# Batched matmul with addend: the weight in one transfer, a strided turn, regrouped stores, and two loads of x ahead of the addends

## The chip, the cores and the metric

The kernel runs on one core of one Trainium2 chip. The metric is device time in microseconds (us); a run's time is a little more than the span of the profiled execution, which goes from the first instruction to the last. Before is given as the median of three runs.

The core has five engines that run their own instruction streams and meet at semaphores: TensorE (PE in the views, with PEld for its weight loads), VectorE (DVE), ScalarE (ACT), GpSimd (POOL) and SyncE (SP), which here issues transfers and computes nothing. Sixteen DMA engines move data between HBM and the core's SBUF.

## The reference

```python
def setup_inputs():
    batch, m, k, n = 16, 512, 1024, 768
    ...
def reference(x, weight, scale, add_value):
    return (scale * np.matmul(x, weight) + add_value).astype(np.float32)
```

All tensors are fp32: x of 16 x 512 x 1024 (33.6 MB), weight of 1024 x 768 (3.1 MB), add_value and the output of 16 x 512 x 768 (25.2 MB each). `scale` is 0.1.

## The kernel before, in words

**Tiles.** The 8192 rows of x are cut into 64 tiles of 128 rows. Tile `t` of a block of 16 takes rows `p * 16 + t` (p the partition), so a transfer of 8 tiles of x is 32768 contiguous bytes in each partition, and one of 8 tiles of addends or results is 24576. "x of 40" means the load that starts at tile 40. `xs` holds 16 tiles of x, `ao` 32 tiles of addends, in which the results are made in place; the weight first lands in the last 8 slots of `ao`.

**The path of a tile.** x lands in `xs` as fp32. ScalarE and GpSimd copy it to bf16 in `va` (L163), four tiles to a move, each engine 8 copies of 32 partitions x 1024 elements to a move; which quarter of the row goes to which partitions prepares the turn. VectorE turns two tiles at once (L178): a transpose of 32 x 32 blocks of fp32 words, each word a pair of bf16, from `va` to `xt`. TensorE multiplies (L208 loads the turned x, L210 streams the weight against it, 8 steps of K, 512 and 256 columns). VectorE finishes two tiles at once (L187): product times scale plus addend, in place in `ao`. SyncE stores from `ao`. The weight is cast to bf16 by VectorE at the start, in two halves (L171). PSUM holds four tiles of products, `xt` four turned tiles, `va` two moves.

**What sets the order.** VectorE's order is written out in `group`: for 8 tiles it waits once for their addends (`a_sem`), then finishes a pair and turns the pair that comes four tiles later, four times over. So a wait for addends holds up the turns behind it. TensorE waits for turned pairs (`turned`) and for finished ones (`made`), GpSimd's and ScalarE's copies for landed x (`x_sem`) and for turned moves (`turned`).

SyncE's order is the list `STREAM`, after a first load of x of 0: "w" the weight, "x" and "a" loads, "o" stores, each with its first tile and its number of tiles. SyncE goes through it in order and waits at each entry for what that needs (`need`, L102): a load of x, that the copies of the 16 tiles before it are made; a load of addends, that the load of addends before it has landed, and that the store of the tiles in its slots has landed; a store, that its tiles are finished, and that the store before the last has landed. All of its transfers go through one queue, in which 16 DMA engines work in the order of issue. "a+" issues nothing.

Tiles 8 and 15 are left out of SyncE's stores: GpSimd stores them (`PAIR`, `store_pair`, L95), in three transfers by partitions (`BY_POOL`), between its copies for tile 31 and those for tile 32. The load of addends that takes their slots waits for these three (`aside_sem`).

`HALF_BLOCK`, `PAST` and `SYNC_AT` place instructions of a stream at a boundary of its code.

Of the kernel before, what the change touches and what calls it, by code (L numbers as in the profile page):

```python
# [8 lines left out]
P = 128  # L9
# [3 lines left out]
A_SLOTS = 32  # L13
# [3 lines left out]
VA_BUFS = 2  # L17
MOVE = 4
AHEAD = 4
HALF_BLOCK, PAST, SYNC_AT = 64, 4, 4  # L20

STREAM = [
# [6 lines left out]
]  # L29
FIRST, ENDING = (0, 8), 48  # L30
PAIR, TURN_AT = slice(8, 16, 7), 2
BY_POOL = [(122, 6), (0, 98), (98, 24)]


# [1 line left out]
def kernel(  # L36
# [9 lines left out]
    bf16 = mybir.dt.bfloat16  # L46
    fp32 = mybir.dt.float32
# [7 lines left out]
    KC = K // (2 * P)  # L55
    KJ = 2 * KC
# [1 line left out]
    x_v = x_f.rearrange("(g p t) k -> p g t k", p=P, t=R)  # L58
    add_v = add_f.rearrange("(g p t) n -> p g t n", p=P, t=R)
    out_v = out_f.rearrange("(g p t) n -> p g t n", p=P, t=R)  # L60
    w_v = weight.rearrange("(c p r) n -> p c (r n)", p=P, r=2)

    def rows(view, s, n):
        assert s // R == (s + n - 1) // R
        return view[:, s // R, s % R:s % R + n, :]
# [3 lines left out]
    xs = nc.alloc_sbuf_tensor("xs", [P, X_SLOTS, K], fp32).ap()  # L69
    const = ctx.enter_context(tc.tile_pool(name="const", bufs=1))  # L70
    ao = const.tile([P, A_SLOTS, N], fp32, name="ao")
    w_bf = const.tile([P, KJ, N], bf16, name="w_bf")
    va = [const.tile([P, MOVE * KC, 4, 64], bf16, name=f"va{i}") for i in range(VA_BUFS)]
    xt = const.tile([P, XT_TILES, KC, P], fp32, name="xt")
    mm = psum.tile([P, MM_BUFS, 1024], fp32, name="mm")

    end_sem = nc.alloc_semaphore("ending")
    w_sem = [tc.alloc_semaphore(f"w{i}") for i in range(2)]
    x_sem = [tc.alloc_semaphore(f"x{i}") for i in range(X_SLOTS // MOVE)]
    a_sem = tc.alloc_semaphore("a")  # L80
    o_sem = [tc.alloc_semaphore(f"o{i}") for i in range(2)]
    aside_sem = tc.alloc_semaphore("aside")
# [5 lines left out]
    W_AT = A_SLOTS - KJ  # L88

    def slot(t):  # L90
        return t % A_SLOTS

    def store_pair(eng, p, n):
        assert PAIR.stop <= R and PAIR.stop <= A_SLOTS
        eng.dma_start(out_v[p:p + n, 0, PAIR, :], ao[p:p + n, PAIR, :]).then_inc(aside_sem, 16)  # L95

    def sync_engine(eng):
        groups, stores, known = 0, [], {}

        def need(sem, value):  # L100
            if known.get(sem, 0) < value:
                eng.wait_ge(sem, value)  # L102
                known[sem] = value

        for at, (op, s, n) in enumerate(STREAM):
            if at == SYNC_AT:
                eng.addr_align(HALF_BLOCK, offset=PAST, max_nops=0)
            last = s + n - 1
            if op == "w":
                dst = ao[:, W_AT + s:W_AT + s + n, :].rearrange("p (c r) n -> p c (r n)", r=2)  # L110
                move, sem = eng.dma_start(dst, w_v[:, s // 2:(s + n) // 2, :]), w_sem[s // 4]
            elif op == "x":
                k = s % X_SLOTS
                if last >= X_SLOTS:
                    moved = 8 * (last + 1 - X_SLOTS) // MOVE
                    need(by_act, moved)
                    need(by_pool, moved)
                move = eng.dma_start(xs[:, k:k + n, :], rows(x_v, s, n))  # L118
                sem = x_sem[k // MOVE]
            elif op == "a":  # L120
                if groups:
                    need(a_sem, 16 * groups)
                if last == A_SLOTS - 1:
                    need(casts, KJ)
                if s <= PAIR.start + A_SLOTS <= last:
                    need(aside_sem, 16 * len(BY_POOL))
                if s >= A_SLOTS:
                    i = next(j for j, (a, b) in enumerate(stores) if a <= last - 1 - A_SLOTS < a + b)
                    need(o_sem[i % 2], 16 * (i // 2 + 1))
                move = eng.dma_start(ao[:, slot(s):slot(s) + n, :], rows(add_v, s, n))  # L130
                sem = a_sem
                groups += 1
            elif op == "a+":
                need(a_sem, 16 * groups)
                eng.sem_inc(a_sem, 16 * (n // G - 1))
                groups += n // G - 1
                continue
            else:
                i = len(stores)
                if i > 1:  # L140
                    need(o_sem[i % 2], 16 * (i // 2))
                need(made, MADE + last + 1)
                move = eng.dma_start(rows(out_v, s, n), ao[:, slot(s):slot(s) + n, :])
                sem = o_sem[i % 2] if s < ENDING else end_sem
                stores.append((s, n))
            move.then_inc(sem, 16)
            if op == "x" and n == 2 * MOVE:
                eng.sem_inc(x_sem[k // MOVE + 1], 16)

    def mover(eng, copy, parity, count, go=None, first=0, turns=T // X_SLOTS):  # L150
        if go is None:
            eng.preload_act_table(mybir.ActivationFunctionType.Copy)  # L152
        with eng.Fori(16 * (first + 1), 16 * (first + turns) + 1, 16) as i:  # L153
            for q in range(X_SLOTS // MOVE):
                eng.wait_ge(x_sem[q], i)
                eng.wait_ge(turned, i + (4 * q - 12) if q < 3 else i)  # L156
                if go is not None:
                    eng.sem_inc(go, 1)  # L158
                k = MOVE * q
                src = xs[:, k:k + MOVE, :].rearrange("p i (c b k) -> p (i c) b k", b=4, k=64)  # L160
                for a in (parity, parity + 2):
                    for b in range(4):
                        copy(va[q % VA_BUFS][32 * b:32 * b + 32, :, a, :],  # L163
                             src[32 * a:32 * a + 32, :, b, :]).then_inc(count, 1)

    def vector_engine(eng):
        ao_g = ao.rearrange("p (g t) n -> p g t n", t=G)

        def cast_w(s, n):
            eng.wait_ge(w_sem[s // 4], 16)  # L170
            eng.tensor_copy(w_bf[:, s:s + n, :], ao[:, W_AT + s:W_AT + s + n, :]).then_inc(casts, n)  # L171

        def turn(move, half, moves=None):
            if half == 0:
                eng.wait_ge(by_act, moves)
                eng.wait_ge(by_pool, moves)  # L176
            q = 2 * half * KC
            eng.transpose(  # L178
                xt[:, 2 * half:2 * half + 2, :, :].rearrange("p i c m -> p (i c m)"),
                va[move % VA_BUFS][:, q:q + 2 * KC, :, :].bitcast(fp32).rearrange("p c a k -> p (c a k)"),  # L180
            ).then_inc(turned, 2)

        def finish(pair, at, products):
            eng.wait_ge(done, products)
            a = ao_g[:, at, 2 * pair:2 * pair + 2, :]
            q = 2 * (pair % 2)
            eng.scalar_tensor_tensor(  # L187
                a, mm[:, q:q + 2, 0:N], float(scale), a,
                op0=mybir.AluOpType.mult, op1=mybir.AluOpType.add).then_inc(made, 2)

        def group(i, at, last):
            eng.wait_ge(a_sem, i)
            for p in range(4):
                finish(p, at, i + (4 * p - 12) if p < 3 else i)
                if p < 2 or not last:
                    turn(1 if p < 2 else 0, p % 2, i + 8 if p == 2 else i)

        cast_w(0, 4)
        cast_w(4, 4)
        turn(0, 0, 8)  # L200
        turn(0, 1)
        with eng.Fori(16, 2 * T, 16) as i:
            group(i, bass.ds((i // 16 + A_SLOTS // G - 1) % (A_SLOTS // G), 1), False)
        s = slot(T - G) // G
        group(2 * T, slice(s, s + 1), True)
# [31 lines left out]
    s, n = FIRST  # L237
# [55 lines left out]
```

## Time and profile before

| | |
|---|---|
| median of 3 runs | 206.99 us (206.83 to 207.0) |
| the profiled execution: time, span | 206.85 us, 205.5 us |
| TensorE busy | 167.5 us of the span, granted clock 0.986 |
| ScalarE, GpSimd, VectorE busy | 134.7, 137.4, 98.0 us |
| bytes moved | 87.04 MB, 424 GB/s over the span |
| HBM read, written | 61.87 MB, 25.17 MB |

Times in the views are us from the start of the span unless marked ns. A row of a timeline has the start, the length, the engine, the line, the operation, what it writes and reads, and how many instructions the row joins; in brackets stands how long the engine was idle before it and what ended that. A row of a group has busy time and mean ns of one, then the idle time just before them. An answer on one line ends with the time from the issue of a transfer to its landing. "SPq" is SyncE issuing transfers. Rows of the chain of waits have start, length and what was running.

### The profile page before, as it was taken

The numbers are of one execution on the slowest core, as the hardware profiler recorded it, in microseconds if no ns is written. First come the engines' busy times: TensorE is split into PE (matmuls) and PEld (weight loads), VectorE is DVE, ScalarE is ACT, GpSimd is POOL, SyncE is SP. The second block draws the span as 40 slices with busy tenths as digits, with TensorE's granted clock in tenths as the row PEclk, the third lists the DMA queues.
The fourth block names the chain that finished last, engine by engine and source line by source line (L and its number), as shares of the span: only waits on it lengthen the run. The fifth ranks groups of instructions, "written<-read, shape, count | busy, mean of one in ns | idle before, by whom it ended". The sixth has DMA issues, their size and how long they took to land.

```text
span 205.5 us, 2223 instructions
## 1 busy us (share of the span) xinstructions
PE 167.5 (82%) x1008; PEld 50.4 (25%) x512; DVE 98.0 (48%) x66; ACT 134.7 (66%) x129; POOL 137.4 (67%) x135
## 2 busy tenths in 40 slices
PE   0000099999999999999999999999999997999900
PEld 0000022233322333223332233332333322333200
DVE  0004525537555555465555555555552853455330
ACT  2049980699999906999999059999991099920000
POOL 0049994699999916999999549999992099930000
PEclk9999999999999999999999999999999999999995
DMA  8989999999999899999999999999999999998997
GB/s 287 427 372 438 440 485 408 392 437 459 446 459 459 357 459 408 408 426 413 455 404 450 431 416 464 434 411 421 440 431 415 437 448 421 493 459 364 423 440 304
DMA packets 4065, 87.04 MB, mean 424 GB/s; under 512 B 480, under 2 KB 480, under 8 KB 1120
## 3 DMA queue, kind: packets, MB, share of 16 engines
q1 hardware_dynamic: 3856, 86.25, 98.1%
q0 software_dynamic: 208, 0.79, 0.9%
q14 instruction: 1, 0.01, 0.0%
HBM read 61.87 MB, written 25.17 MB: 424 GB/s over the span
## 4 chain that ended last, share of the span: by engine, by line
DMA 38%; PE 36%; POOL 10%; ACT 5%; issue 4%; DVE 3%; SPq 1%; POOLq 0%; DVEq 0%; ACTq 0%
PE mm L210 36%; DMA out_dram<-ao 22%; DMA xs<-in_x_dram 15%; POOL va L163 9%; ACT va L163 5%; DVE xt L178 2%; DVE ao L187 1%; POOL out_dram L95 1%; SPq L130 0%; SPq L118 0%; DVEq L176 0%; SPq L102 0%; POOLq L156 0%; POOLq L158 0%; POOLq L153 0%
## 5 line engine op out<-in xcount | busy, mean ns | idle before, releaser
L210 PE MATMUL mm<-w_bf,xt 128*128 128x256 bf16 (+1 forms) x1008 | 167.5, 327 | 28.0 <-DVE xt L178 27.1
L163 POOL CAST va<-xs 32x1024 bf16<-32x1024 f32 x128 | 135.2, 1056 | 44.2 <-DMA xs<-in_x_dram 36.8
L163 ACT CAST va<-xs 32x1024 bf16<-32x1024 f32 x128 | 133.4, 1042 | 45.2 <-DMA xs<-in_x_dram 42.2
L187 DVE SCALAR_TENSOR_TENSOR ao<-mm,ao 128x1536 f32 (+1 forms) x32 | 56.2, 1756 | 72.9 <-PE mm L210 68.9
L208 PEld LDWEIGHTS <-xt 128*128 128x128 bf16 x512 | 50.4, 98 | 144.6 <-issue 116.6
L178 DVE STREAM_TRANSPOSE xt<-va 128x1024 f32<-128x1024 f32 x32 | 39.4, 1234 | 8.4 <-POOL va L163 6.3
L171 DVE CAST w_bf<-ao 128x3072 bf16<-128x3072 f32 x2 | 4.5, 2240 | 18.1 <-DMA ao<-in_weight_dram 18.1
L152 ACT ACT_TABLE_LOAD x1 | 1.3, 1283 | 1.3 <-SPq L242 1.3
L95 POOL DMA_DIRECT2D out_dram<-ao x3 | 2.0, 672 | 0.0
L274 POOL MEMSET const-float32-0.0<- 128x1 f32 x1 | 0.1, 98 | 0.2 <-issue 0.2
L274 POOL MEMSET const-bfloat16-1.0<- 128x1 bf16 x1 | 0.1, 101 | 0.0
L274 POOL MEMSET const-float32-1.0<- 128x1 f32 x1 | 0.1, 98 | 0.0
L274 POOL MEMSET const-uint8-127<- 128x1 uint8 x1 | 0.1, 98 | 0.0
## 6 DMA issues: line engine op xcount, KB each, us to landing
xs<-in_x_dram SPq DMA_DIRECT2D x7, 4096.0 KB, 20.9
ao<-in_add_value_dram SPq DMA_DIRECT2D x6, 3072.0 KB, 15.7
out_dram<-ao SPq DMA_DIRECT2D x3, 3072.0 KB, 27.4
ao<-in_add_value_dram SPq DMA_DIRECT2D x1, 6144.0 KB, 24.2
out_dram<-ao SPq DMA_DIRECT2D x1, 6144.0 KB, 31.2
out_dram<-ao SPq DMA_DIRECT2D x1, 4608.0 KB, 14.9
xs<-in_x_dram SPq DMA_DIRECT2D x2, 2048.0 KB, 21.0
ao<-in_weight_dram SPq DMA_DIRECT2D x2, 1536.0 KB, 16.8
```

The costliest lines, as they stand in the source:

```text
L95: eng.dma_start(out_v[p:p + n, 0, PAIR, :], ao[p:p + n, PAIR, :]).then_inc(aside_sem, 16)
L152: eng.preload_act_table(mybir.ActivationFunctionType.Copy)
L163: copy(va[q % VA_BUFS][32 * b:32 * b + 32, :, a, :], src[32 * a:32 * a + 32, :, b, :]).then_inc(count, 1)
L171: eng.tensor_copy(w_bf[:, s:s + n, :], ao[:, W_AT + s:W_AT + s + n, :]).then_inc(casts, n)
L178: eng.transpose(xt[:, 2 * half:2 * half + 2, :, :].rearrange("p i c m -> p (i c m)"), va[move % VA_BUFS][:, q:q + 2 * KC, :, :].bitcast(fp ...
L187: eng.scalar_tensor_tensor(a, mm[:, q:q + 2, 0:N], float(scale), a, op0=mybir.AluOpType.mult, op1=mybir.AluOpType.add).then_inc(made, 2)
L208: eng.ldweights(x_j, tile_position=(0, 0))
L210: m = eng.add_instruction(mybir.InstMatmult(start_tensor_calc=(j == 0), stop_tensor_calc=(j == KJ - 1), tile_size=(P, P), tile_position=(0 ...
L274: nc = _bacc.Bacc("TRN2", target_bir_lowering=False, num_devices=1)
```

## The change

Five edits:

- the weight goes in one transfer, and with another assignment of its rows: partition p holds rows 8p to 8p + 7 (24576 contiguous bytes) instead of two rows out of each of four blocks (four pieces of 6144 bytes). Both casts wait for the one semaphore;
- for that, x is dealt out differently: a copy takes 256 elements in a row of each of 4 tiles instead of 16 runs of 64, and the turn gathers with a step of 4 fp32 words (16 bytes) what the four chunks of K need. What it writes lies as before;
- GpSimd stores tiles 14 and 15 (6144 contiguous bytes in a partition) instead of 8 and 15 (two pieces of 3072);
- SyncE stores tiles 0 to 13 in one transfer instead of 0 to 7 and 9 to 14 in two; a load of addends into one of these slots waits for the one store;
- in `STREAM`, x of 40 stands ahead of the addends of 32, and x of 48 ahead of the addends of 40. `SYNC_AT` is one less, as there is one entry less ahead of the same place.

```diff
-HALF_BLOCK, PAST, SYNC_AT = 64, 4, 4
+HALF_BLOCK, PAST, SYNC_AT = 64, 4, 3
 STREAM = [
-    ("w", 0, 4), ("w", 4, 4), ("a", 0, 8),
+    ("w", 0, 8), ("a", 0, 8),
     ("x", 8, 8), ("a", 8, 8), ("x", 16, 8), ("a", 16, 16), ("x", 24, 8),
-    ("x", 32, 8), ("a+", 16, 16), ("o", 0, 8), ("o", 9, 6), ("a", 32, 8), ("x", 40, 8),
-    ("a", 40, 8), ("x", 48, 8), ("o", 16, 8), ("o", 24, 8), ("a", 48, 8), ("x", 56, 4),
+    ("x", 32, 8), ("a+", 16, 16), ("o", 0, 14), ("x", 40, 8), ("a", 32, 8),
+    ("x", 48, 8), ("a", 40, 8), ("o", 16, 8), ("o", 24, 8), ("a", 48, 8), ("x", 56, 4),
...
-PAIR, TURN_AT = slice(8, 16, 7), 2
+PAIR, TURN_AT = range(14, 16), 2
...
-    w_v = weight.rearrange("(c p r) n -> p c (r n)", p=P, r=2)
+    w_v = weight.rearrange("(p r) n -> p r n", r=KJ)
...
-    va = [const.tile([P, MOVE * KC, 4, 64], bf16, name=f"va{i}") for i in range(VA_BUFS)]
+    va = [const.tile([P, MOVE, 4, 2 * P], bf16, name=f"va{i}") for i in range(VA_BUFS)]
...
-    w_sem = [tc.alloc_semaphore(f"w{i}") for i in range(2)]
+    w_sem = tc.alloc_semaphore("w")
...
                 if s >= A_SLOTS:
-                    i = next(j for j, (a, b) in enumerate(stores) if a <= last - 1 - A_SLOTS < a + b)
+                    t = max(t for t in range(s - A_SLOTS, last + 1 - A_SLOTS) if t not in PAIR)
+                    i = next(j for j, (a, b) in enumerate(stores) if a <= t < a + b)
                     need(o_sem[i % 2], 16 * (i // 2 + 1))
...
-                src = xs[:, k:k + MOVE, :].rearrange("p i (c b k) -> p (i c) b k", b=4, k=64)
+                src = xs[:, k:k + MOVE, :].rearrange("p i (b k) -> p i b k", b=4)
...
-            eng.wait_ge(w_sem[s // 4], 16)
+            eng.wait_ge(w_sem, 16)
...
-            q = 2 * half * KC
+            i = slice(2 * half, 2 * half + 2)
             eng.transpose(
-                xt[:, 2 * half:2 * half + 2, :, :].rearrange("p i c m -> p (i c m)"),
-                va[move % VA_BUFS][:, q:q + 2 * KC, :, :].bitcast(fp32).rearrange("p c a k -> p (c a k)"),
+                xt[:, i, :, :].rearrange("p i c (a m) -> p i c a m", a=4),
+                va[move % VA_BUFS][:, i, :, :].bitcast(fp32).rearrange("p i a (k c) -> p i c a k", c=KC),
             ).then_inc(turned, 2)
```

More of the change, by code (lines that the diff above doesn't have):

```diff
@@ L94, in store_pair @@
         assert PAIR.stop <= R and PAIR.stop <= A_SLOTS
-        eng.dma_start(out_v[p:p + n, 0, PAIR, :], ao[p:p + n, PAIR, :]).then_inc(aside_sem, 16)
+        eng.dma_start(out_v[p:p + n, 0, PAIR.start:PAIR.stop, :], ao[p:p + n, PAIR.start:PAIR.stop, :]).then_inc(aside_sem, 16)
     def sync_engine(eng):
@@ L109, in sync_engine @@
             if op == "w":
-                dst = ao[:, W_AT + s:W_AT + s + n, :].rearrange("p (c r) n -> p c (r n)", r=2)
-                move, sem = eng.dma_start(dst, w_v[:, s // 2:(s + n) // 2, :]), w_sem[s // 4]
+                move, sem = eng.dma_start(ao[:, W_AT + s:W_AT + s + n, :], w_v[:, s:s + n, :]), w_sem
             elif op == "x":
```

## Prediction

> **What bounds the kernel now.** I read the page first: the strip of DMA by slices, the DMA queues, the chain that ended last, the groups.
>
> ```profile
> DMA  8989999999999899999999999999999999998997
> DMA packets 4065, 87.04 MB, mean 424 GB/s; under 512 B 480, under 2 KB 480, under 8 KB 1120
> q1 hardware_dynamic: 3856, 86.25, 98.1%
> DMA 38%; PE 36%; POOL 10%; ACT 5%; issue 4%; DVE 3%; SPq 1%; POOLq 0%; DVEq 0%; ACTq 0%
> L210 PE MATMUL mm<-w_bf,xt 128*128 128x256 bf16 (+1 forms) x1008 | 167.5, 327 | 28.0 <-DVE xt L178 27.1
> L178 DVE STREAM_TRANSPOSE xt<-va 128x1024 f32<-128x1024 f32 x32 | 39.4, 1234 | 8.4 <-POOL va L163 6.3
> ```
>
> The packets of SyncE's queue fill 98.1% of what 16 engines could give, and no slice is under 7 tenths. TensorE waits some 26 us at the start and about 1 us later. Two candidates then, so the next view is the busy time by stretches (length, PE, PEld, DVE, ACT, POOL, clock, DMA share, GB/s), cut where loads of x were seen to land.
>
> ```profile
> 2.00:78.60 76.60, 52.34 (x309) 15.73 (x158) 33.12 (x22) 50.66 (x49) 52.47 (x48) 1.00 0.99 426
> 78.60:120.40 41.80, 41.59 (x255) 12.54 (x129) 23.36 (x16) 33.36 (x32) 35.05 (x35) 1.00 1.00 426
> 120.40:159.20 38.80, 38.64 (x237) 11.73 (x120) 20.45 (x14) 33.36 (x32) 33.09 (x32) 1.00 1.00 430
> ```
>
> The transfers never rest, at 426 to 430 GB/s in every stretch, whichever engine is waiting. So the end is set by bytes: 87.04 MB, which the change doesn't alter. TensorE only has to finish early enough that the last two stores (tiles 48 to 59, and 60 to 63) are issued before the queue runs dry. How early it is stands in the timelines of SyncE and TensorE and in the answers on line 143, one store each, each issue with its time to landing below it (tiles 32 to 47, 48 to 59, 60 to 63; the last row is of the chain).
>
> ```profile
> 174.49 20.97 PE L210 MATMUL mm<-w_bf,xt 128*128 128x512 bf16 x126 [1.13 <-DVE xt L178]
> 159.64 0.42 SPq L143 DMA_DIRECT2D out_dram<-ao  x1
> DMA to landing us min/median/max: 31.2/31.2/31.2
> 186.96 10.78 SPq L143 DMA_DIRECT2D out_dram<-ao  x2
> DMA to landing us min/median/max: 14.9/14.9/14.9
> 197.41 0.33 SPq L143 DMA_DIRECT2D out_dram<-ao  x1
> DMA to landing us min/median/max: 8.1/8.1/8.1
> 0.74 12.05 DMA xs<-in_x_dram
> ```
>
> Landings: 159.64 + 31.2 = 190.8, 186.96 + 14.9 = 201.9, 197.41 + 8.1 = 205.5, the span's end. The middle store took 11.0 us for 4.72 MB, 429 GB/s, so nothing was missing between them. What would a store cost that meets an empty queue? The nearest row is the very first load: 12.05 us from issue to landing for 4.19 MB (128 x 8192 fp32), of which 9.8 us is moving at 429 GB/s, so some 2.3 us to start and to end. I estimate from it that the store of tiles 48 to 59 must be issued by 190.8 - 2.3 = 188.5, and the last by 201.9 - 2.3 = 199.6. They were issued 1.5 and 2.2 us ahead. That spare, not TensorE's busy share, is what the change can use up.
>
> **The change, part by part.** I work on the profiled execution: span 205.5, time 206.85, so 1.35 us lie around the span; the median of the three runs, 206.99, is 0.14 above it.
>
> *Weight in one transfer.* Rows of the timelines of VectorE, SyncE and GpSimd:
>
> ```profile
> 16.65 2.31 DVE L171 CAST w_bf<-ao 128x3072 bf16<-128x3072 f32 x1 [16.65 <-DMA ao<-in_weight_dram]
> 20.40 2.17 DVE L171 CAST w_bf<-ao 128x3072 bf16<-128x3072 f32 x1 [1.44 <-DMA ao<-in_weight_dram]
> 24.69 2.37 DVE L178 STREAM_TRANSPOSE xt<-va 128x1024 f32<-128x1024 f32 x2 [2.12 <-ACT va L163]
> 27.64 0.33 SPq L130 DMA_DIRECT2D ao<-in_add_value_dram  x1
> 13.04 20.27 POOL L163 CAST va<-xs 32x1024 bf16<-32x1024 f32 x16 [12.60 <-DMA xs<-in_x_dram]
> 16.31 4.64 POOL L163 CAST va<-xs 32x1024 bf16<-32x1024 f32 x3
> 78.84 17.45 POOL L163 CAST va<-xs 32x1024 bf16<-32x1024 f32 x16 [6.30 <-DMA xs<-in_x_dram]
> ```
>
> The halves were seen 20.40 - 16.65 = 3.75 us apart, so the weight takes 7.50 us in pieces of 6144 bytes. The first addends, as many bytes in pieces of 24576, landed when SyncE went on at 27.64: 7.24 us. The weight now has that shape: 0.26 us saved, and as the queue never rests, it is saved at the end too. The first cast can't start at 16.65 any more; both follow at about 20.2. That could cost TensorE its start, but GpSimd's copies share the bill: undisturbed they follow each other every 17.45/16 = 1.09 us (the row at 78.84), and the row of three (4.64 us instead of 3.2) shows 1.4 us of standing still behind a cast. From 13.04 on, with no cast in their way, GpSimd has done six of the eight copies that the first turn needs by 20.2 and is in the seventh, until 20.6. Then come two casts of some 1.6 us (20.40 to 22.57 less the 0.55 in which the cast waited for a copy) and the eighth copy, one behind the other: 20.6 + 3.2 + 1.1 = 24.9. The first turn starts 0.2 us later than at 24.69. Bounds: 0 (the trace's order kept) to 1.0 (one copy more behind the casts).
>
> *The copies* keep 1024 elements; runs of 64 become runs of 256. Nothing saved or lost: ScalarE's and GpSimd's 128 copies are no bound. A tenth of a copy either way, 16 copies to a load of x, is 1.7 us on the issue of the next load, and that has cover below.
>
> *The turn strided.* 32 turns of 1.234 us now read every fourth fp32, 16 bytes apart, where they read in a row. No row of this trace has an operation with such a step. The nearest is the turn itself, 1.23 us, and that is my value; the far end is twice it, 2.47 us. VectorE's timeline tells what that does in the steady state:
>
> ```profile
> 116.44 1.76 DVE L187 SCALAR_TENSOR_TENSOR ao<-mm,ao 128x1536 f32 x1 [2.42 <-PE mm L210]
> 121.51 1.76 DVE L187 SCALAR_TENSOR_TENSOR ao<-mm,ao 128x1536 f32 x1 [2.16 <-PE mm L210]
> ```
>
> A pair of tiles takes TensorE 121.51 - 116.44 = 5.1 us, and finishing and turning need 1.76 + 1.23, or 1.76 + 2.47 = 4.2: covered either way. The turn's length counts only where TensorE waits for a turn: at the start, and behind the late addends below.
>
> [...]
>
> *Stores of tiles 0 to 13 in one, 14 and 15 by GpSimd.* The same bytes; 14 tiles in pieces of 43008 bytes instead of 24576 and 18432, and GpSimd's 6144 in one piece instead of two. The stretch with these stores ran at 426 GB/s, the next at 430: 41.8 x 4/430 = 0.4 us is all that can come back. I take 0.1; ends 0 and 0.4.
>
> *x of 40 and 48 ahead of addends 32 and 40.*
>
> ```profile
> 73.13 0.82 SPq L143 DMA_DIRECT2D out_dram<-ao  x2
> DMA to landing us min/median/max: 22.8/25.5/28.2
> 96.02 0.34 SPq L130 DMA_DIRECT2D ao<-in_add_value_dram  x1
> 116.40 0.33 SPq L130 DMA_DIRECT2D ao<-in_add_value_dram  x1
> 116.82 0.39 SPq L118 DMA_DIRECT2D xs<-in_x_dram  x1
> 117.32 0.84 SPq L143 DMA_DIRECT2D out_dram<-ao  x2
> 96.23 2.01 POOL L95 DMA_DIRECT2D out_dram<-ao  x3
> 98.29 17.44 POOL L163 CAST va<-xs 32x1024 bf16<-32x1024 f32 x16
> 120.68 1.03 POOL L163 CAST va<-xs 32x1024 bf16<-32x1024 f32 x1 [4.95 <-DMA xs<-in_x_dram]
> ```
>
> The stores of 0 to 7 and 9 to 14 went out at 73.13 and, second, 73.5, and landed at 95.9 and 73.5 + 28.2 = 101.7; the one store of 14 lands at about 101.4, 0.35 us of savings taken off. x of 40 waits for the copies of 24 to 31, done at 78.84 + 17.45 = 96.3, and is issued then, as now; that store still has 5 us to run, so the queue stays full. Addends 32 now wait for all 14 tiles, so they are issued at 101.4 instead of 96.02 and queue behind x of 40. Of these two loads and GpSimd's stores, the last landed at 120.5 (copy at 120.68); now the addends are last of the same bytes: 120.5 less 0.35 saved = 120.1. x of 48 waits for copies done at 98.29 + 17.44 = 115.7 and goes out there; it needs 120.1 - 2.3 = 117.8, so 2.1 us of cover. Addends 40 wait for addends 32, so go out at 120.2 behind it, not at 116.40. Behind these on SyncE stand only the stores of 16 to 31, which used to follow at 117.32 and have x of 48 ahead of them in the queue until about 129. No gap.
>
> But who waits for addends 32?
>
> ```profile
> 159.59 1.76 DVE L187 SCALAR_TENSOR_TENSOR ao<-mm,ao 128x1536 f32 x1 [3.97 <-DMA ao<-in_add_value_dram]
> 161.26 1.24 DVE L178 STREAM_TRANSPOSE xt<-va 128x1024 f32<-128x1024 f32 x1
> 159.26 0.33 SPq L130 DMA_DIRECT2D ao<-in_add_value_dram  x1
> 164.75 8.61 PE L210 MATMUL mm<-w_bf,xt 128*128 128x512 bf16 x51
> ```
>
> VectorE finished tiles 32 and 33 at 116.44; now it can't before 120.1. Behind that, on the same engine, stands the turn of tiles 36 and 37, for which TensorE is ready at 121.45 (it ends tiles 34 and 35 just before the row at 121.51). What a late landing costs, the rows around 159 show for addends 48: seen by SyncE at 159.26, turn done at 161.26 + 1.24 = 162.5, 3.25 us on. So here 120.1 + 3.25 = 123.35, and TensorE stands 1.9 us. It swallows the 0.2 us of the start. Later TensorE has 1.13 us to give: now it ends tile 55 at 164.75 + 8.61 = 173.36 and waits for x of 56 until 174.49. Shifted: 173.36 + 1.9 = 175.3, so the last eight tiles come 0.8 us later. The stores go out at 187.8 and 198.2 against 188.5 - 0.35 = 188.15 and 199.25. Covered, with 0.35 us spare at the first.
>
> **Sum:** -0.26 (weight) - 0.1 (stores) + 0 (TensorE's 1.9 us, hidden) = 206.85 - 0.36 = 206.5 for the profiled execution, 206.6 for the median.
>
> **The rivals.**
>
> *The turn takes twice as long.* For it: the step, the only one in the kernel that skips 16 bytes at each element; against it: nothing in the trace. [...] TensorE then starts 1.4 us late, which the wait for addends 32 swallows, and the turn behind them ends at 124.6: 3.15 us of standing, 2.0 left at the end. The store of 48 to 59 goes out at 189.0 against 188.15: the queue is empty for 0.85 us. 206.5 + 0.85 = 207.35, on the median's scale 207.5: slower. It decides from a turn of 1.23 + 0.35 = 1.6 us on; above 1.23 + 0.35 + 0.36, about 1.9, the loss exceeds the gain.
>
> *The stores give back more.* If all 0.4 us of that stretch returns, 206.99 - 0.26 - 0.4 = 206.3. For it: 426 against 430 GB/s; against it: nothing ties the difference to the shape of the stores.
>
> *The covers are thinner than I think.* If addends 32 land 1 us later or the spare of 188.5 is 1 us less, the end moves by what exceeds 0.35, 0.65 us, and with both 1.65: 207.3 to 208.3 on the median's scale. Against it: 2.3 us is from a cold load, the longest case.
>
> *It does nothing:* the pieces' size was not what made the weight slow; then 207.0.
>
> **How the numbers follow.** Forecast 0.45 (206.4 to 206.8 on the median's scale, by the ends of the stores' term), turn slower 0.27, stores give more 0.13, thin covers 0.08, nothing 0.07. About 0.2% (0.4 us, so below 206.58 or above 207.40) is what a measurement of this kernel can tell from no change. Faster: a bit under half of the forecast, 0.20, and the stores' case, 0.13, with 0.02 of the rest: 0.35. Slower: 0.18 of the turn's 0.27 and 0.06 of the thin covers: 0.24. Same: 0.41. Range 206.2 to 207.7: it takes in the stores' end and the doubled turn, and leaves out the worse covers.
>
> **What the profile after would show.** Right: no slice with DMA under 7 tenths between first and last; one cast seen near 20.2 and the first turn near 24.9; VectorE waiting for addends some 3.7 us near 120, TensorE 1.9 us; 1.13 us before the last eight tiles gone; the last two stores issued near 187.8 and 198.2. Wrong: a turn far from 1.23 us, x of 48 issued after 117.8, or a gap between the landings of the last three stores.

## The result, and the profile after

The changed kernel takes 208.44 us (median of 6 runs, 208.30 to 208.78) against 207.00 (206.83 to 207.06): 1.0074 times the time before, 95% interval 1.0061 to 1.0086. It is slower by 1.4 us; the forecast was 206.6, with a range up to 207.7. The profiled execution took 208.4 us, with a span of 207.1.

The page of after, the lines that answer to those of before:

```profile
DMA  7999999999999999999899999999999999998995
DMA packets 3521, 87.04 MB, mean 420 GB/s; under 512 B 448, under 2 KB 448, under 8 KB 576
q1 hardware_dynamic: 3312, 86.25, 97.4%
PE 35%; DMA 23%; DVE 2%; issue 1%; DVEq 0%; SPq 0%
L210 PE MATMUL mm<-w_bf,xt 128*128 128x256 bf16 (+1 forms) x1008 | 168.5, 328 | 29.4 <-DVE xt L178 28.5
L178 DVE STREAM_TRANSPOSE xt<-va 128x1024 f32<-128x1024 f32 x32 | 65.6, 2054 | 0.3 <-POOL va L163 0.3
```

The bytes are the same, in 544 packets fewer, and the chain of waits still runs through TensorE and the transfers, as before. SyncE's queue fills 97.4% instead of 98.1%, of a longer span. The turn takes 2054 ns instead of 1234. But TensorE stands only 1.4 us longer in all (29.4 against 28.0), and the strip differs mainly in its last slices: 9, 9, 5 at the end where before has 9, 9, 7. So the time went at the very end. The stretches there (length, busy times of the engines, clock, DMA share, GB/s), first before, then after. A view counts a piece of a transfer whole in the stretch in which it begins, so a share over 1 and the dip behind it belong together:

```profile
203.00:204.00 1.00, 0.00 (x0) 0.00 (x0) 0.00 (x0) 0.00 (x0) 0.00 (x0) 0.50 1.06 455
204.00:205.00 1.00, 0.00 (x0) 0.00 (x0) 0.00 (x0) 0.00 (x0) 0.00 (x0) 0.50 0.35 148
205.00:206.00 1.00, 0.00 (x0) 0.00 (x0) 0.00 (x0) 0.00 (x0) 0.00 (x0) 0.50 0.00 0
```

```profile
203.00:204.00 1.00, 0.00 (x0) 0.00 (x0) 0.00 (x0) 0.00 (x0) 0.00 (x0) 0.50 1.10 467
204.00:205.00 1.00, 0.00 (x0) 0.00 (x0) 0.00 (x0) 0.00 (x0) 0.00 (x0) 0.50 0.79 332
205.00:206.00 1.00, 0.00 (x0) 0.00 (x0) 0.00 (x0) 0.00 (x0) 0.00 (x0) 0.50 0.06 25
206.00:207.00 1.00, 0.00 (x0) 0.00 (x0) 0.00 (x0) 0.00 (x0) 0.00 (x0) 0.50 0.03 12
```

A share of 0.06 is 1/16: what begins from 205 on is the work of a single DMA engine. 25 GB/s over 1 us are two of the last store's pieces of 12288 bytes, and 12 is one more. The other fifteen are done or in their last piece (the last of them ends at 205.3), and this one begins three more pieces of 0.46 us, 1.4 us of work, the last of which ends at 206.55. Before ends with no such tail.

Is that engine late only there? Each engine closes its share of a transfer with a record of 4 bytes (368 on SyncE's queue in after, 16 to each of its 23 transfers), so the trace's single records tell how far the first and the last of the 16 are from the middle one at every landing. Us behind (+) or ahead (-) of the median engine, worked out from these records:

```
landing of              before              after            sync_all (below)
                     first   last       first   last       first   last
the first store      -0.18  +0.40       -0.26  +0.43       -0.26  +0.34
x of 40, addends 32  -1.51  +0.37       -1.82  +0.45       -0.26  +0.39   (the later one)
tiles 16 to 23       -0.76  +0.38       -1.82  +0.72       -0.27  +0.63
tiles 24 to 31       -0.76  +0.38       -1.82  +0.96       -0.27  +0.91
tiles 32 to 47       -0.88  +0.27       -1.45  +1.49       -0.33  +1.73
tiles 60 to 63       -0.88  +0.34       -0.08  +1.59       -0.33  +2.01
```

In after the last engine falls behind by 0.2 us in a store of 8 tiles and by 0.42 us in one of 16, but by only 0.11 us over the four loads between them (+0.96 to +1.07). From tiles 16 on it is so far apart that its pieces can be followed in a row (medians): those of 24576 bytes in the stores of 16 to 31 take 0.937 us on it and 0.912 on the others, those of 49152 bytes in the store of 32 to 47 take 1.867 and 1.815. Eight of these are 8 x 0.052 = 0.42 us, what the table shows. So one DMA engine is some 3% slower than the others in these stores; the pieces of 12288 bytes of the last store take 0.46 us on it as on the others. In before there is no engine that ends late: the theory to be tested is that there the slow one has a head start, because GpSimd's stores of tiles 8 and 15 gave it few pieces.

### The profile page after: what moved, and what is told of

Its sections match the earlier page's. It is cut to its first block, busy times and chain, and to the rows that moved or that the text cites. A ratio compares the mean times of both kernels' runs of the same rounds, so it can differ in the third digit from the quotient of the medians.

```text
span 207.1 us, 2221 instructions
## 1 busy us (share of the span) xinstructions
PE 168.5 (81%) x1008; PEld 50.5 (24%) x512; DVE 123.9 (60%) x66; ACT 134.8 (65%) x129; POOL 137.0 (66%) x135
## 3 DMA queue, kind: packets, MB, share of 16 engines
q1 hardware_dynamic: 3312, 86.25, 97.4%
HBM read 61.87 MB, written 25.17 MB: 420 GB/s over the span
## 4 chain that ended last, share of the span: by engine, by line
PE 35%; DMA 23%; DVE 2%; issue 1%; DVEq 0%; SPq 0%
PE mm L210 35%; DMA out_dram<-ao 13%; DMA ao<-in_add_value_dram 9%; DVE xt L178 1%; DVE ao L187 1%; DVEq L187 0%; DVEq L184 0%; SPq L102 0%
## 5 line engine op out<-in xcount | busy, mean ns | idle before, releaser
L210 PE MATMUL mm<-w_bf,xt 128*128 128x256 bf16 (+1 forms) x1008 | 168.5, 328 | 29.4 <-DVE xt L178 28.5
L178 DVE STREAM_TRANSPOSE xt<-va 128x1024 f32<-128x1024 f32 x32 | 65.6, 2054 | 0.3 <-POOL va L163 0.3
## 6 DMA issues: line engine op xcount, KB each, us to landing
out_dram<-ao SPq DMA_DIRECT2D x1, 6144.0 KB, 31.6
```

The lines of the kernel that those rows point to most:

```text
L178: eng.transpose(xt[:, i, :, :].rearrange("p i c (a m) -> p i c a m", a=4), va[move % VA_BUFS][:, i, :, :].bitcast(fp32).rearrange("p i a ( ...
L210: m = eng.add_instruction(mybir.InstMatmult(start_tensor_calc=(j == 0), stop_tensor_calc=(j == KJ - 1), tile_size=(P, P), tile_position=(0 ...
```

## The experiments

The theory (**late engine**): what decides is how many of GpSimd's 128 pieces of 6144 bytes (0.234 us each by the trace) the slow engine gets. Its rivals: the **strided turn** makes TensorE late; the **order** of loads and the regrouped store let the queue run dry before the last stores; the **shape** of the large stores is slower. Before ran beside every group of runs, with medians of 206.89 to 206.96.

**layout_only.** The weight, copies and strided turn of after, all else as before (against after):

```diff
-    ("x", 32, 8), ("a+", 16, 16), ("o", 0, 14), ("x", 40, 8), ("a", 32, 8),
-    ("x", 48, 8), ("a", 40, 8), ("o", 16, 8), ("o", 24, 8), ("a", 48, 8), ("x", 56, 4),
+    ("x", 32, 8), ("a+", 16, 16), ("o", 0, 8), ("o", 9, 6), ("a", 32, 8), ("x", 40, 8),
+    ("a", 40, 8), ("x", 48, 8), ("o", 16, 8), ("o", 24, 8), ("a", 48, 8), ("x", 56, 4),
...
-PAIR, TURN_AT = range(14, 16), 2
+PAIR, TURN_AT = slice(8, 16, 7), 2
```

> Weight in one transfer, its row assignment, the copies and the strided turn as in the changed kernel; stores and order of loads as before. Theory 1 (TensorE's end): the slow turn (2.05 us) and the late addends together push the store of tiles 48 to 59 past the moment at which the queue runs dry. Here the addends of 32 land at about 110 again, so the slow turn costs TensorE only about 1 us at the start, the 1.13 us ahead of the last eight tiles swallow it, and the saved 0.25 us stays: 206.7 to 206.9. Theory 2 (one late DMA engine): GpSimd's regrouped stores, or their splitting, leave one of the 16 DMA engines 1.3 us behind the others, and it alone sets the end. Here the stores are as before: 206.7 to 206.9 too. A time near 208 would say that the layout costs by itself, against both.

**no_layout.** The reverse: stores, pair and order of after, with the weight in two transfers, the copies and the turn of before.

```diff
-    ("w", 0, 8), ("a", 0, 8),
+    ("w", 0, 4), ("w", 4, 4), ("a", 0, 8),
...
-    va = [const.tile([P, MOVE, 4, 2 * P], bf16, name=f"va{i}") for i in range(VA_BUFS)]
+    va = [const.tile([P, MOVE * KC, 4, 64], bf16, name=f"va{i}") for i in range(VA_BUFS)]
```

> The regrouped stores and the new order alone; weight in two, turn in a row (1.23 us). Theory 1: addends 32 land at about 120.8, TensorE stands some 2 us instead of 2.9, the store of 48 to 59 is issued near 188.5, about when the queue runs dry: 206.8 to 207.2. Theory 2: the late engine is still there, since the stores are: 208.0 to 208.4, with one DMA engine at work for more than a microsecond after the others at the end.

Measured: layout_only 207.02 us, ratio 0.9997 [0.9988, 1.0006]; no_layout 208.49, 1.0070 [1.0057, 1.0083]. The turn's group and the end, first of layout_only, then of no_layout:

```profile
L177 DVE STREAM_TRANSPOSE xt<-va 128x1024 f32<-128x1024 f32 x32 | 65.4, 2046 | 1.4 <-POOL va L162 1.4
205.00:206.00 1.00, 0.00 (x0) 0.00 (x0) 0.00 (x0) 0.00 (x0) 0.00 (x0) 0.50 0.00 0
```

```profile
L179 DVE STREAM_TRANSPOSE xt<-va 128x1024 f32<-128x1024 f32 x32 | 39.4, 1235 | 3.5 <-ACT va L164 2.1 <-POOL va L164 1.4
205.00:206.00 1.00, 0.00 (x0) 0.00 (x0) 0.00 (x0) 0.00 (x0) 0.00 (x0) 0.50 0.06 25
206.00:207.00 1.00, 0.00 (x0) 0.00 (x0) 0.00 (x0) 0.00 (x0) 0.00 (x0) 0.50 0.03 12
```

The slow turn costs nothing by itself, and without it the whole loss is there, single engine and all. The strided turn falls as the cause.

**old_stores.** After with the stores and the pair of before; the new order of loads stays.

```diff
-    ("x", 32, 8), ("a+", 16, 16), ("o", 0, 14), ("x", 40, 8), ("a", 32, 8),
+    ("x", 32, 8), ("a+", 16, 16), ("o", 0, 8), ("o", 9, 6), ("x", 40, 8), ("a", 32, 8),
...
-PAIR, TURN_AT = range(14, 16), 2
+PAIR, TURN_AT = slice(8, 16, 7), 2
```

> The changed kernel with the stores as before (tiles 8 and 15 by GpSimd, 0 to 7 and 9 to 14 by SyncE), but the new layout and the new order of loads. Theory 1: addends 32 still come behind x of 40 and land near 120.8, the turn still takes 2.05 us, so the store of 48 to 59 still goes out near 189.4: 208.2 to 208.5. Theory 2: the late engine is gone: 206.9 to 207.4, though the store of 48 to 59 still goes out near 189.4.

Measured: 207.24, ratio 1.0031 [1.0012, 1.0049]. The 12 values fall in two groups, seven at 206.77 to 207.31 and five at 208.11 to 208.43. The profiled execution is of the lower group. Its late stores are issued at 189.60, later than in after:

```profile
189.60 10.78 SPq L142 DMA_DIRECT2D out_dram<-ao  x2
...
188.00:189.00 1.00, 1.00 (x8) 0.29 (x3) 1.00 (x1) 0.00 (x0) 0.00 (x0) 1.00 1.59 688
189.00:190.00 1.00, 1.00 (x8) 0.29 (x3) 1.00 (x2) 0.00 (x0) 0.00 (x0) 1.00 0.11 49
190.00:191.00 1.00, 1.00 (x7) 0.29 (x3) 1.00 (x1) 0.00 (x0) 0.00 (x0) 1.00 1.38 590
205.00:206.00 1.00, 0.00 (x0) 0.00 (x0) 0.00 (x0) 0.00 (x0) 0.00 (x0) 0.50 0.04 12
```

The 0.11 isn't a queue run dry: few pieces begin between 189 and 190, because those of 1.8 us that began before still run. By their records the engines were busy for 0.94 of that stretch and 0.89 of the next, so they stood for 0.2 us on average, and this execution took 207.31 us. So a store of tiles 48 to 59 that goes out at 189.6, later than in after (189.40), costs a few tenths, not 1.4 us: the order alone isn't the cause. What makes the upper group isn't shown.

**one_pair_store.** After, with the pair in one transfer of 128 partitions, eight pieces to each engine if they are dealt evenly.

```diff
-BY_POOL = [(122, 6), (0, 98), (98, 24)]
+BY_POOL = [(0, 128)]
```

> The changed kernel, but GpSimd stores tiles 14 and 15 in one transfer of 128 partitions instead of three (6, 98, 24), so that each DMA engine gets 8 of its 128 pieces. Theory 1: nothing changes for TensorE: 208.2 to 208.5. Theory 2, if the late engine comes from an uneven share of pieces: 207.0 to 207.5. If the engine is slow by itself in stores, only the 0.5 us go that two pieces too many are worth: 207.9.

Measured: 208.00, ratio 1.0055 [1.0043, 1.0067], and one engine alone from 205 to 206:

```profile
205.00:206.00 1.00, 0.00 (x0) 0.00 (x0) 0.00 (x0) 0.00 (x0) 0.00 (x0) 0.50 0.06 25
206.00:207.00 1.00, 0.00 (x0) 0.00 (x0) 0.00 (x0) 0.00 (x0) 0.00 (x0) 0.50 0.00 0
```

Shorter than after by 0.44 us, two pieces' worth (2 x 0.234), and still 1.1 slower than before. An even share isn't the fastest.

**sync_all, share_moved, other_engine.** Three edits of before alone, so none of the change is in them. sync_all lets SyncE store tiles 8 to 15 too, so that every engine gets an equal share, as of SyncE's other transfers (in before all 16 lie within 0.45 us of each other at each landing ahead of the first store); share_moved issues GpSimd's three transfers in another order; other_engine cuts them elsewhere.

```diff
-    ("x", 32, 8), ("a+", 16, 16), ("o", 0, 8), ("o", 9, 6), ("a", 32, 8), ("x", 40, 8),
+    ("x", 32, 8), ("a+", 16, 16), ("o", 0, 8), ("o", 8, 8), ("a", 32, 8), ("x", 40, 8),
...
-BY_POOL = [(122, 6), (0, 98), (98, 24)]
+BY_POOL = []
```

> The kernel before, but SyncE stores tiles 0 to 7 and 8 to 15 itself and GpSimd stores nothing, so every DMA engine gets the same. Theory 1: no change or a little faster, 206.7 to 207.0 (GpSimd has 2 us more). Theory 2: the slow engine has its full share, 8 pieces' worth instead of 3, 5 x 0.234 = 1.2 us later: 207.7 to 208.2.

```diff
-BY_POOL = [(122, 6), (0, 98), (98, 24)]
+BY_POOL = [(0, 98), (98, 24), (122, 6)]
```

> The kernel before; only the order of GpSimd's three transfers differs: 98, 24, 6 partitions instead of 6, 98, 24. Same bytes, same pieces, same waits. Theory 1 (TensorE's end) and any theory of sizes: no change, 206.9 to 207.1. Theory 2 (one late DMA engine): one of the 16 engines is slower than the rest in every later store, and was given only 3 of the 128 pieces; in this order another pair of engines gets the 3, and that engine 9, six more at 0.234 us, so 1.4 us: 207.9 to 208.5, with one engine at work alone at the end.

```diff
-BY_POOL = [(122, 6), (0, 98), (98, 24)]
+BY_POOL = [(122, 6), (0, 120), (120, 2)]
```

> The kernel before, GpSimd's transfers with 6, 120 and 2 partitions. Dealt out in turn, as theory 2 supposes (6 engines one each, the next 15 engines eight each, then two one each), exactly one engine is left with 2 pieces, the later one of the two that have 3 now. If that is the slow engine: 206.6 to 207.0, possibly a little faster than before. If the slow one is the other of the two, it gets 9: 208.0 to 208.5. Theory 1: no change.

Measured: sync_all 208.00, ratio 1.0048 [1.0035, 1.0061]; share_moved 208.32, 1.0069 [1.0056, 1.0082]; other_engine 208.37, 1.0063 [1.0050, 1.0076]. The last stretches of share_moved, and of other_engine:

```profile
205.00:206.00 1.00, 0.00 (x0) 0.00 (x0) 0.00 (x0) 0.00 (x0) 0.00 (x0) 0.50 0.06 25
206.00:207.00 1.00, 0.00 (x0) 0.00 (x0) 0.00 (x0) 0.00 (x0) 0.00 (x0) 0.50 0.00 0
```

```profile
205.00:206.00 1.00, 0.00 (x0) 0.00 (x0) 0.00 (x0) 0.00 (x0) 0.00 (x0) 0.50 0.06 25
206.00:207.00 1.00, 0.00 (x0) 0.00 (x0) 0.00 (x0) 0.00 (x0) 0.00 (x0) 0.50 0.03 12
```

share_moved is the plainest run of all: the same three transfers of the same bytes in another order cost the whole 1.4 us. No shape of a store, no order of loads and no turn has changed there. And in sync_all, with all shares equal, the lateness itself is seen (the table above): the last engine goes from +0.34 to +2.01 us. Not all of that came in stores: 0.5 us of it in addends 56, the load just ahead of the store of tiles 32 to 47.

**pair_13_15.** After, with the pair 13 and 15 instead of 14 and 15: again two pieces of 3072 in a partition, as in before.

```diff
-    ("x", 32, 8), ("a+", 16, 16), ("o", 0, 14), ("x", 40, 8), ("a", 32, 8),
+    ("x", 32, 8), ("a+", 16, 16), ("o", 0, 13), ("o", 14, 1), ("x", 40, 8), ("a", 32, 8),
...
-PAIR, TURN_AT = range(14, 16), 2
+PAIR, TURN_AT = slice(13, 16, 2), 2
```

> The changed kernel, but GpSimd stores tiles 13 and 15 (two pieces of 3072 bytes in a partition, as before the change) and SyncE 0 to 12 in one and 14 by itself. If the regrouping as such or the one long store costs: 208.2 to 208.5. Theory 2 in its sharper form, that the two pieces in a partition being one run changes how the transfers are dealt out to the engines: the slow engine has 3 pieces again, 206.9 to 207.4, as in the changed kernel with the old stores.

Measured: 207.16, ratio 1.0025 [1.0007, 1.0043]; eight values at 207.04 to 207.36, three at 208.33 to 208.64. The turn and the order are those of after, and tiles 0 to 12 go in one store; the profiled execution (of the lower group) issues its late store almost as late, and has no engine alone at the end:

```profile
189.27 10.78 SPq L143 DMA_DIRECT2D out_dram<-ao  x2
...
204.00:205.00 1.00, 0.00 (x0) 0.00 (x0) 0.00 (x0) 0.00 (x0) 0.00 (x0) 0.50 0.76 320
205.00:206.00 1.00, 0.00 (x0) 0.00 (x0) 0.00 (x0) 0.00 (x0) 0.00 (x0) 0.50 0.00 0
```

The medians of this and of after (208.44) are 1.28 us apart, and what differs between them is whether the pair is contiguous, with the SyncE store of tile 14 that goes with it. That three of eleven executions are as slow as after stays open, as with old_stores: the two kernels have the new order of loads and the old kind of pair in common. In both, the upper group has the lower granted clocks (0.983 to 0.986, against 0.986 to 0.993 in the lower group), but before runs at 0.980 to 0.989 without it, so the clock alone doesn't make the group.

**five_first, layout_five.** If the count of pieces on one engine decides, another cut that gives it two (by the count below) must be as fast as before (five_first), and on top of layout_only it might keep the 0.25 us that the weight saves (layout_five).

```diff
-BY_POOL = [(122, 6), (0, 98), (98, 24)]
+BY_POOL = [(123, 5), (0, 120), (120, 3)]
```

> The kernel before, GpSimd's transfers with 5, 120 and 3 partitions: the run with 6, 120 and 2 moved on by one engine. Dealt out in turn (5 engines one each, the next 15 eight each, the last three one each), the engine left out of the 120 is now the earlier of the two that have 3 pieces before the change, so by the run with 6, 120 and 2 it is the slow one: it has 2 pieces, and the time falls back to 206.7 to 207.1, from 208.4 there. If it is not the place of the small share but the three transfers' sizes that count, this kernel is as slow as that one: 208.0 to 208.5.

> The same with the new layout (weight in one transfer, strided turn), stores and order of loads as before: the version that should beat both, if the 0.25 us saved on the weight reaches the end: 206.6 to 206.9. If the slower load ahead of the first store takes it back, as in the layout's own run, 206.9 to 207.1.

Measured: five_first 206.98, ratio 1.0002 [0.9993, 1.0011]; layout_five 207.00, 1.0009 [0.9999, 1.0020]. The first came out as the theory has it, the second gave no gain: no version that was run beats before.

How are the pieces dealt? The trace's records carry no engine numbers, but on one engine a piece begins 3 or 4 ns before the last one ends, so the records from x of 32 on can be linked into 16 chains. Where two ends fall together more than one link fits, so the links were drawn many times; where the draws differ, both counts are given. In every trace a single chain has the long pieces of the store of tiles 32 to 47 (1.85 to 1.87 us on average, against 1.815), on all three chips on which the experiments ran. Of GpSimd's 128 pieces it has 3 in before, layout_only, old_stores and pair_13_15 (the last two in their lower groups), 10 in after and no_layout, 8 in one_pair_store, 8 or 9 in share_moved and other_engine, 2 in five_first, 2 or 4 in layout_five. In after, no_layout, one_pair_store, share_moved, other_engine and sync_all this chain is the one that ends last; in nearly all draws for early_store too, where it has 3 to 5.

In part the records show it: in before GpSimd's pieces begin in four rounds of 14, 1.14 us apart, from 104.06 on, in after in five rounds of 14, 1.44 us apart, from 104.58 on. So 14 engines were at these pieces in each round, and two were not. Whether 120 partitions go out in a like way on 15, as the expectations of other_engine and five_first suppose, isn't shown; the counts on the slow chain, 8 or 9 and 2, are what that would give it. By the linked records:

```
kernel           transfers       pieces on the slow chain   us
five_first       5, 120, 3        2                         206.98
before           6, 98, 24        3                         206.9 to 207.0
one_pair_store   128              8                         208.00
sync_all         (SyncE's own)    8 (estimate)              208.00
share_moved      98, 24, 6        8 or 9                    208.32
other_engine     6, 120, 2        8 or 9                    208.37
after            6, 98, 24       10                         208.44
no_layout        6, 98, 24       10                         208.49
```

The 8 of sync_all is a sixteenth of the 128 pieces' bytes, which are part of SyncE's store there. From 8 to 10 pieces the time grows by 0.45 us, 0.22 a piece, beside the 0.234 us that a piece takes; 2 and 3 pieces give the same time, so there the other engines share in setting the end. That the pieces lie otherwise in after than in before, with the same three cuts, is seen at the landings as well: in after two engines are 1.82 and 1.80 us ahead of the median at that of addends 32; in before, at that of x of 40, the first two are 1.51 and 0.94 ahead.

**early_store.** Why did layout_only not keep the weight's 0.25 us? In it and in after, x of 32 takes longer than other loads of x. By the records the median engine needs 9.71 us for x of 24 in each, but for x of 32, the last load before the first store, 9.90 in before, 10.41 in after and 10.54 in layout_only. This run puts the first store one load earlier in before.

```diff
-    ("x", 32, 8), ("a+", 16, 16), ("o", 0, 8), ("o", 9, 6), ("a", 32, 8), ("x", 40, 8),
+    ("o", 0, 8), ("x", 32, 8), ("a+", 16, 16), ("o", 9, 6), ("a", 32, 8), ("x", 40, 8),
```

> The kernel before with its first store (tiles 0 to 7) ahead of x of 32 instead of behind it. In all profiles so far the DMA engines are slower for some two microseconds from 85 us on, near the end of the load ahead of the first store, and the load of x of 32 takes 10.0 to 10.7 us instead of 9.7. If that belongs to the change from loads to the first store, it now comes near 76, and x of 32 takes 9.7; if it belongs to the moment, it stays at 85. The time itself: within 0.3 us of before on either reading, since the bytes and the shares are the same.

Measured: 207.39, ratio 1.0026 [1.0001, 1.0051], a little more than the 0.3 us that were expected at most; two of the ten values, 209.3 and 210.19, lie far above the rest. Now x of 24, which stands ahead of the store, takes 10.18 us and x of 32 takes 9.91, and the stretch in which few bytes move (393 GB/s over these two rows together) is there, where before had full ones:

```profile
74.00:76.00 2.00, 2.00 (x14) 0.63 (x7) 0.00 (x0) 0.00 (x0) 0.00 (x0) 1.00 1.42 524
76.00:78.00 2.00, 2.00 (x15) 0.59 (x6) 1.89 (x2) 0.00 (x0) 0.00 (x0) 1.00 0.66 262
```

So the slow moment belongs to the passage from loads to the first store, not to a time or a load. How long it is, and why, isn't shown: kernels with the old layout have up to 10.35 us there (other_engine), those with the new one 10.24 (layout_five) to 10.60 (old_stores), with one trace of each.

## Why the prediction was wrong

The timelines of after (start, length, engine, line), in the order of the prediction's steps:

```profile
20.18 4.59 DVE L171 CAST w_bf<-ao 128x3072 bf16<-128x3072 f32 x2 [20.18 <-DMA ao<-in_weight_dram]
24.70 3.90 DVE L178 STREAM_TRANSPOSE xt<-va 128x1024 f32<-128x1024 f32 x2
27.40 0.33 SPq L130 DMA_DIRECT2D ao<-in_add_value_dram  x1
96.12 0.33 SPq L117 DMA_DIRECT2D xs<-in_x_dram  x1
102.01 0.33 SPq L130 DMA_DIRECT2D ao<-in_add_value_dram  x1
115.25 0.33 SPq L117 DMA_DIRECT2D xs<-in_x_dram  x1
120.86 0.33 SPq L130 DMA_DIRECT2D ao<-in_add_value_dram  x1
121.19 1.76 DVE L187 SCALAR_TENSOR_TENSOR ao<-mm,ao 128x1536 f32 x1 [4.60 <-DMA ao<-in_add_value_dram]
124.92 72.98 PE L210 MATMUL mm<-w_bf,xt 128*128 128x512 bf16 x441 [1.78 <-DVE xt L178]
189.40 10.78 SPq L143 DMA_DIRECT2D out_dram<-ao  x2
199.84 0.33 SPq L143 DMA_DIRECT2D out_dram<-ao  x1
```

- *Weight, -0.26 at the end.* The mechanism was right, and the gain was lost on the way. The weight is seen at 20.18, and the next issue is 0.24 us earlier (27.40 for 27.64). But x of 32 lands at 73.55 + 15.2 = 88.75 against 72.62 + 16.0 = 88.6 before: the passage to the first store took it back, and layout_only, which has this weight, takes 207.02. That "as the queue never rests, it is saved at the end too" failed here.
- *First turn at 24.9.* 24.70: right, at the lower bound.
- *The turn, "1.23 us, and that is my value".* The size was off: 2.05, two thirds of the way to the far end. That end and the 0.27 of its rival were the author's estimates, as no row of before has such a step. But the turn decided nothing: layout_only has the slow turn at 207.02.
- *"Stores of tiles 0 to 13 in one, 14 and 15 by GpSimd. The same bytes [...] I take 0.1; ends 0 and 0.4."* This is the step that failed. Measured: a loss of 1.3 us (after against pair_13_15, 208.44 and 207.16). Both ends were gains, with no reason to exclude a loss. The prediction counted the sixteen engines as one queue that ends when the bytes are moved; but a transfer ends with its last engine, and one engine is slower (1.867 against 1.815 us a piece). GpSimd's uneven pieces evened that out, which no view of means over 16 engines shows.
- *The loads moved.* Near to what was forecast: x of 40 at 96.12 (96.3), addends 32 issued at 102.01 (101.4) and seen at 120.86 (120.1), x of 48 at 115.25 (115.7). TensorE stands 1.78 us (1.9), and the 1.13 us before the last eight tiles are gone.
- *Last stores at 187.8 and 198.2, deadline 188.15.* They came at 189.40 and 199.84: 0.8 from the turn, 0.8 from the later addends 32. The answer on line 143 gives the landings of the last three stores, issued at 160.56, 189.40 and 199.84:

```profile
DMA to landing us min/median/max: 31.6/31.6/31.6
...
DMA to landing us min/median/max: 14.0/14.0/14.0
...
DMA to landing us min/median/max: 7.2/7.2/7.2
```

160.56 + 31.6 = 192.2, then 203.4 and 207.0. Read as I read them in before, they seem to show a queue that starts late from 192.2; but a landing is that of the last of the 16 engines (tiles 32 to 47: the middle one is done at 190.21, the last at 191.69, and the landing is at 192.2). By the deadline the loss at 189.40 would be 1.25 us, and the rival of the doubled turn would seem to have come true. But no_layout issues the same store 0.8 us earlier and is as slow; old_stores issues it 0.2 us later and takes 207.24. The records of after say it outright: the late engine closed its share of tiles 32 to 47 at 191.69, when the next store had been out for 2.3 us and others had been at work on it since 190.25, and from there its pieces follow each other without a gap to the end. So the late issue didn't move the end, the deadline was too strict for it, and that rival is refuted.
- *Rivals.* "It does nothing" and "The stores give back more" are refuted as well; "The covers are thinner than I think" came nearest in time (207.3 to 208.3), by another cause. That a cold load is the longest case, which spoke against it, rests on one comparison: in before its first piece begins 1.0 us after its issue, and in after that of the store issued at 189.40 begins 0.84 us after. Missing was a rival in which the engines' shares change.

What is shown: share_moved, five_first and pair_13_15 tie the 1.3 us to GpSimd's pieces, the windows to one engine alone at the end, and the linked records show that this is the slow one, with 3 of the pieces in before and 10 in after. What isn't shown: by what rule the pieces are dealt to the engines. Open: why an engine is 3% slower in stores, and the two groups of values of old_stores and pair_13_15.

## What to carry to other kernels

When a kernel is bound by its transfers, ask of the last microseconds how many of the 16 engines are still at work: a share of 0.06 is one. (A short stretch must be read with its neighbours, as a piece counts where it begins.) The shares that an uneven or second queue gives to each engine are part of the balance, so an edit that changes their shape, their order or their contiguity needs a term of its own, with a loss as one end (here 1.4 us for the order alone, in share_moved). And a chain of waits that names TensorE or a late issue is no proof; undo that part alone and see whether the time comes back.

## What was not expected of the hardware

- One of the 16 DMA engines takes some 3% longer for pieces of stores (1.867 against 1.815 us for 49152 bytes). Over all stores that would be 25.17 MB / 16 / 49152 bytes x 0.052 = 1.66 us. In loads it fell behind by less in after, 0.11 us over four, but by 0.5 us in one of sync_all. Every trace has one such engine (1.85 to 1.87 us on average), on three chips.
- The same three GpSimd transfers in another order move the end by 1.4 us (206.94 to 208.32).
- The load just ahead of the first store is 0.2 to 0.9 us slower than its like (9.90 to 10.60 us in thirteen traces, against 9.71).
- A VectorE transpose of 1024 fp32 elements per partition that reads with a step of 16 bytes takes 2.05 us instead of 1.23.
